# A hybrid encoder layer on one core: filter network and normalised input in a fixed order at the start

## The chip, the cores and the metric

The kernel runs on one core of one Trainium2 chip. The core has a matrix engine (TensorE, PE in the profile, with its weight loads as PEld), a vector engine (VectorE, DVE), an activation engine (ScalarE, ACT), a general engine (GpSimd, POOL) and a queue that issues the DMAs here (SyncE, SP). Each works through its own instructions in the order in which they were written down at build time, and waits on semaphores for the others. The metric is the device time of one execution in microseconds (us); lower is better.

## The reference

One layer, applied to a prompt of 1024 tokens and to a sample of 512, both of width 1024, all in float32:

```python
h = rmsnorm(x, norm_g)
z = h @ w_in                                   # 1024 -> 4096
hy_in, hy_gate, att_qkv, att_gate = split(z)
x0, x1, vv = split(short_conv(hy_in))
kfilt = hyena_filter(L, ...)                   # depends on L and the weights only
y_hy  = rmsnorm(x0 * long_conv(x1 * vv, kfilt, hy_bias)) * silu(hy_gate)
y_att = rmsnorm(neighbourhood_attention(q, k, v)) * silu(att_gate)
return x + concat([y_hy, y_att]) @ w_out

def hyena_filter(L, ...):                      # a small network of positions
    z = [t, cos(f w), -sin(f w)]               # 33 features
    h = sin(fr1 * (z @ w1 + b1))
    h = sin(fr2 * (h @ w2 + b2))
    h = (h @ w3) * exp(-t |deltas|)            # forward and backward halves
```

## The kernel before, in words

Products in full float32 precision are made of three faster ones: each operand is split into a rounded high part and a low remainder (`whi`, `wlo` for weights, `hThi`, `hTlo` for the normalised, transposed input), and high-high, high-low and low-high are added. A weight block `wraw` (128x1024) is loaded by SP, its two halves rounded by ScalarE into `whi` and, in all stages, subtracted by GpSimd into `wlo` (line 365).

The order of the work within an engine is not that of the code: a scheduler sorts the instructions by priority and by a simulation of the engines at build time, and writes one list for each engine. A block under `high_priority(n)` goes ahead; a block under `manual_schedule(engines=...)` keeps, on the named engine, the order in which the code issues it.

The start does this for the prompt, in two segments of 512 tokens. Four 128x1024 tiles `x` arrive; ScalarE sums their squares (`xsq`, line 229); VectorE takes an inverse root of the four sums (`rsqrt`: a seed and three Newton steps on 128x4 elements, tiles `rs_h`, `rs_y`, `rs_t`); VectorE scales the four `x` (line 79); TensorE transposes 128x128 squares of them into PSUM banks, ScalarE rounds a bank into `hThi` and VectorE subtracts it into `hTlo` (line 75). The projections (line 404) of a segment then run, three matmuls to each of 8 depth blocks and 4 token blocks, first `k` and `q`, then `v` and the gates.

Beside it the filter network runs: features `z_p`, `z_s` times `w1` (line 164), a sine argument reduced to one turn by VectorE (tiles `arg`, `n`), a sine on ScalarE (line 178), the second layer the same way, and a split into `hm`. Then VectorE adds up transform matrices (`dftm` from `km`, `fc`) and splits `w3`. The next step, the K phase, multiplies `hm` by `w3` (line 552) and by the decay tables `dec` into `xk`, and transforms the result (tiles `zc`) into the filters' spectra, which are stored as `K_p` and `K_s`. It runs woven with the projections. Meanwhile the sample's rows `px` are normalised, turned into `hl`, and stored as `hT`. After it come the long convolution of the prompt, the prompt's attention with the sample's convolution, the sample's attention and the output product.

Of the kernel before, what the change touches and what calls it, by code (L numbers as in the profile page):

```python
# [9 lines left out]
F32 = mybir.dt.float32  # L10
F32R = mybir.dt.float32r
I32 = mybir.dt.int32
AF = mybir.ActivationFunctionType
ALU = mybir.AluOpType
AX = mybir.AxisListType

P = 128
D = 1024
KC = 8
# [15 lines left out]
def f32(ap):  # L35
    return ap.bitcast(F32)


class Group:
    def __init__(self, name, L, x, out, z2, dec, tw0):  # L40
        self.name, self.L, self.x, self.out, self.z2, self.dec = name, L, x, out, z2, dec
        self.nt = L // P
        self.rows = L // GW
        self.B = 2 * L // P
        self.half = self.B // 2
        self.tw0 = tw0
        self.nseg = L // 512


class Kernel:  # L50
# [49 lines left out]
    def setup(self):  # L100
        nc, io, ctx = self.nc, self.io, self.ctx
        g = self.gp = ctx.enter_context(self.pool("const"))
        self.wp = ctx.enter_context(self.pool("w"))
        self.w_pools = itertools.repeat(self.wp)
        self.w_round = itertools.repeat(nc.scalar.copy)
        self.psum_cm, self.pp = {}, {}
        self.w_pos, self.w_raw, self.w_ready, self.w_bufs = 0, [], [], 4
        self.dr = ctx.enter_context(self.pool("dr", space=bass.MemoryType.DRAM))

        self.ident = g.tile([P, P], F32, name="ident")  # L110
        make_identity(nc, self.ident)
        self.ones = g.tile([P, 1], F32, name="ones")
        nc.gpsimd.memset(self.ones, 1.0)
        self.pc = g.tile([P, 70], F32, name="pc")
        self.dma(self.pc, io["pconst"])
        o = 0
        names = [("norm_g", 8), ("cw0", 12), ("cw1", 12), ("cw2", 12), ("cb", 12), ("on_hy", 4), ("on_att", 4),
                 ("qg", 1), ("kg", 1), ("b1", 1), ("fr1", 1), ("b2", 1), ("fr2", 1)]
        self.v = {}
        for n, w in names:  # L120
            self.v[n] = self.pc[:, o:o + w]
            o += w
        self.gq = g.tile([P, 1], F32, name="gq")
        nc.scalar.mul(out=self.gq, in_=self.v["qg"], mul=-0.125)
        self.fc = g.tile([P, 4, P], F32, name="fc")
        self.F = {n: self.fc[:, i] for i, n in enumerate(["M1f", "M2f", "M1i", "M2i"])}

        self.A_d, self.ga_d, self.v_d, self.K_d, self.qk_d = {}, {}, {}, {}, {}
        self.sum_d = self.dr.tile([self.P_.L, D], F32, name="sum")
        self.hT_d = [self.dr.tile([P, KC, self.S_.L], F32, name=f"hT{a}") for a in range(2)]  # L130
        for G in (self.P_, self.S_):
            self.A_d[G.name] = [self.dr.tile([P, G.L], F32, name=f"A_{G.name}{i}") for i in range(8)]
            self.ga_d[G.name] = [self.dr.tile([P, G.L], F32, name=f"ga_{G.name}{i}") for i in range(4)]
            self.K_d[G.name] = [self.dr.tile([P, 2 * G.half + 1, P], F32, name=f"K_{G.name}{i}") for i in range(4)]
            self.qk_d[G.name] = {(n, i): self.dr.tile([G.L, 256], F32, name=f"{n}_{G.name}{i}") for n in "qk" for i in range(2)}
            nr = 16 if G.name == "p" else 9
            self.v_d[G.name] = [[self.dr.tile([nr * 40, 4, P], F32, name=f"v_{G.name}{i}{hf}") for hf in range(2)] for i in range(2)]

    def mlp_setup(self, fl, mp):
        io = self.io  # L140
        self.hm, self.z, self.w12 = {}, {}, []
        self.w3 = [fl.tile([P, HW], F32R, name=f"w3{n}") for n in ("f", "b", "lof", "lob")]
        for nm in ("w1", "w2"):
            self.w12.append(mp.tile([io[nm].shape[0], P], F32, name=nm))
        for G in (self.P_, self.S_):
            self.hm[G.name] = [fl.tile([P, G.L], F32R, name=f"hm{d}_{G.name}") for d in range(2)]
            self.z[G.name] = mp.tile([66, G.L], F32, name=f"z_{G.name}")

    def mlp_load(self):
        for w, nm in zip(self.w12, ("w1", "w2")):  # L150
            self.dma(w, self.io[nm])
        for G in (self.P_, self.S_):
            self.dma(self.z[G.name], G.z2)

    def filters_mlp(self, G, mp):
        nc = self.nc
        w1, w2 = self.w12
        h = self.z[G.name]
        for layer, (w, b, fr) in enumerate(((w1, "b1", "fr1"), (w2, "b2", "fr2"))):
            nxt = None if layer else mp.tile([P, G.L], F32, name=f"h1_{G.name}")  # L160
            for s in range(G.nseg):
                sl = slice(s * 512, (s + 1) * 512)
                ps = self.bank("ml")
                nc.tensor.matmul(ps, lhsT=w, rhs=h[:, sl], start=True, stop=True)
                arg = mp.tile([P, 512], F32, name="arg", bufs=2)
                self.ts(arg, ps, self.v[b], ALU.add, self.v[fr], ALU.mult)
                n = mp.tile([P, 512], F32, name="n", bufs=2)
                magic = 12582912.0
                self.ts(n, arg, 1.0 / TWO_PI, ALU.mult, magic, ALU.add)
                self.ts(n, n, magic, ALU.subtract)  # L170
                c1 = 6.28125
                c2 = 0.0019350051879882812
                c3 = TWO_PI - c1 - c2
                self.stt(arg, n, -c1, arg)
                self.stt(arg, n, -c2, arg)
                self.stt(arg, n, -c3, arg)
                self.ts(arg, arg, 3.1415925, ALU.min, -3.1415925, ALU.max)
                nc.scalar.activation(out=nxt[:, sl] if nxt else arg, in_=arg, func=AF.Sin)
                if layer:
                    self.stack([t[:, sl] for t in self.hm[G.name]], arg)  # L180
            h = nxt
            yield

    def stack(self, out, src):

# [16 lines left out]
    def rsqrt(self, pool, ss, n, scale, name):  # L202
# [6 lines left out]
        self.ts(y.bitcast(I32), y.bitcast(I32), -1, ALU.mult, 0x5F3759DF, ALU.add)  # L209
        for _ in range(3):  # L210
            self.mul(t, y, y)
            self.mul(t, t, h)
            self.ts(t, t, -0.5, ALU.mult, 1.5, ALU.add)
            self.mul(y, y, t)
        return y


    def x_norm(self, G, xp, ahead):

        nc = self.nc  # L220
        G.xs = []
        for s in range(G.nseg):
            ss = xp.tile([P, 4], F32, name="ss", bufs=2)
            for j in range(4):
                tt = s * 4 + j
                x = xp.tile([P, D], F32, name="x", bufs=G.nt)
                self.dma(x, G.x[tt * P:(tt + 1) * P, :])
                sq = xp.tile([P, D], F32, name="xsq", bufs=1)
                nc.scalar.activation(out=sq, in_=x, func=AF.Square, accum_out=ss[:, j:j + 1])
                G.xs.append(x)  # L230
                if ahead:
                    ahead.pop(0)()
            r = self.rsqrt(xp, ss, 4, 1.0 / D, "x")
            for j in range(4):
                x = G.xs[s * 4 + j]
                self.ts(x, x, r[:, j:j + 1])

    def x_turn(self, G, hps):

        nc = self.nc  # L240
        G.hi = [p.tile([P, KC, 512], F32R, name=f"hThi_{G.name}") for p in hps]
        G.lo = [p.tile([P, KC, 512], F32R, name=f"hTlo_{G.name}") for p in hps]
        for s in range(G.nseg):
            for k in range(KC):
                ps = self.bank()
                for j in range(4):
                    nc.tensor.transpose(out=ps[:, j * P:(j + 1) * P], in_=G.xs[s * 4 + j][:, k * P:(k + 1) * P], identity=self.ident)
                gk = self.v["norm_g"][:, k:k + 1]
                nc.scalar.activation(out=G.hi[s][:, k], in_=ps, func=AF.Copy, scale=gk)
                self.stt(G.lo[s][:, k], ps, gk, f32(G.hi[s][:, k]), ALU.subtract)  # L250

    def x_pre(self, G, pool):

# [99 lines left out]
    def issue_w(self):  # L353
# [6 lines left out]
        for u in range(2):  # L360
# [1 line left out]
            lo = pool.tile([P, 512], F32R, name="wlo", bufs=4)  # L362
            r = raw[:, u * 512:(u + 1) * 512]
            next(self.w_round)(out=hi, in_=r)  # L364
            nc.gpsimd.tensor_tensor(out=lo, in0=r, in1=f32(hi), op=ALU.subtract)  # L365
            self.w_ready.append((key, hi, lo))

    def take_w(self, key):
# [762 lines left out]
    def run(self):  # L1131
# [30 lines left out]
        sc, sp = opn("stage")  # L1162
        mc, mp = opn("mlp")
        self.mlp_setup(fl, mp)
        with self.tc.high_priority(4000):
            self.x_norm(Gp, xp, [lambda: None] * 3 + [self.issue_w] + [lambda: None] * 3 + [self.issue_w])
            self.x_turn(Gp, (hp0, hp1))
        self.mlp_load()
        for _ in zip(self.filters_mlp(Gp, mp), self.filters_mlp(Gs, mp)):
            pass  # L1170
        self.w3_load(mp)
        self.dft_load(self.fc, self.io["fconst"].rearrange("p (n a) c -> p n a c", a=2), sp, "fc")
        self.dft = self.dft_mats(kd, self.io["kmat"], range(1, 8), sp, ("km0", "km1"))
# [211 lines left out]
```

## Time and profile before

| what | us |
|---|---|
| three runs | 1089.95, 1091.8, 1094.8 |
| their median | 1091.8 |
| the profiled execution | 1090.92 |
| its span between first and last instruction | 1089.1 |
| TensorE busy in the span | 1003.6 |
| VectorE / ScalarE / GpSimd busy | 800.1 / 463.1 / 415.5 |

The profiled execution takes 1.8 us more than its span, and 0.9 us less than the median. TensorE is busy for 92% of the span; the first of the 40 slices (27 us each) shows it busy for three tenths and the second for eight. A busy share counts an instruction until its modelled end, so that consecutive matmuls overlap; the rate at which they start is read from their start times.

### The profile page before, as it was taken

What the parts mean: (1) busy time and instruction counts of PE and PEld (TensorE: products, weight loads), DVE (VectorE), ACT (ScalarE), POOL (GpSimd) and SP (SyncE); (2) the same over time, 40 slices, a digit from 0 to 9 for tenths busy, and PEclk for the clock granted to TensorE, in tenths of its full rate; (3) what the DMA queues carried; (4) which work ended last, traced back from release to release, by engine and by line L of the source; (5) the groups of instructions that cost most, each with busy time, mean ns of one, the idle gap of its engine ahead of it and who ended that gap; (6) DMA issues with size and microseconds to landing.
All of it is one profiled execution on the core that took longest, in us unless ns stands there. A gap on an engine that the chain in (4) does not pass through costs nothing.

```text
span 1089.1 us, 18072 instructions
## 1 busy us (share of the span) xinstructions
PE 1003.6 (92%) x6444; PEld 906.6 (83%) x6444; DVE 800.1 (73%) x2134; ACT 463.1 (43%) x958; POOL 415.5 (38%) x336
## 2 busy tenths in 40 slices
PE   3898999988999999999989999987989989899997
PEld 2698999977788888888877887876968879899987
DVE  5997779552157767967559999887967977587874
ACT  6453334233331323122124565655747653476530
POOL 2032332112142323123256344354254356784651
PEclk9999999999999999999989999999999999999999
DMA  8226372756312121212483354435544478966522
GB/s 299 69 78 195 119 235 91 242 161 241 109 39 80 58 62 58 67 54 92 173 240 106 94 145 130 129 100 168 141 133 115 132 237 263 295 183 211 173 72 97
DMA packets 112216, 154.84 MB, mean 142 GB/s; under 512 B 7953, under 2 KB 80475, under 8 KB 111615
## 3 DMA queue, kind: packets, MB, share of 16 engines
q1 hardware_dynamic: 112127, 153.69, 45.3%
q8 instruction: 51, 0.84, 0.3%
q14 instruction: 38, 0.31, 0.1%
HBM read 110.35 MB, written 43.32 MB: 141 GB/s over the span
## 4 chain that ended last, share of the span: by engine, by line
PE 48%; DVE 27%; DMA 12%; issue 5%; ACT 4%; SPq 2%; POOL 1%; POOLq 0%; DVEq 0%; ACTq 0%
PE bank L391 25%; PE bank L1094 7%; PE bank L443 3%; PE bank L404 3%; DMA dec<-in_dec_p_dram 2%; PE bank L1012 2%; SPq L60 2%; DVE zc L63 2%; DMA v_p<-vg 2%; DMA v_s<-vg 2%; PE bank L445 2%; PE bank L444 2%; DVE s_sb L981 2%; PE bank L1003 2%; DVE s L63 1%
## 5 line engine op out<-in xcount | busy, mean ns | idle before, releaser
L365 POOL TENSOR_TENSOR wlo<-wraw,whi 128x512 fp32r<-128x512 f32 x160 | 233.7, 1464 | 514.3 <-ACT whi L364 322.5
L391 PE MATMUL bank<-hThi_p,whi 128*128 128x512 f32 x320 | 126.8, 396 | 3.9 <-DVE vg L63 3.2
L391 PE MATMUL bank<-hThi_p,wlo 128*128 128x512 f32 x320 | 126.7, 396 | 0.0
L391 PE MATMUL bank<-hTlo_p,whi 128*128 128x512 f32 x320 | 126.3, 395 | 0.0
L404 PE MATMUL bank<-whi,hThi_p 128*128 128x256 f32 x384 | 111.6, 293 | 6.3 <-DVE vg L63 3.2
L1094 PE MATMUL bank<-whi,hi 128*128 128x256 f32 x384 | 111.6, 292 | 6.0 <-ACT oo L1106 2.6
L1094 PE MATMUL bank<-whi,lo 128*128 128x256 f32 x384 | 110.7, 292 | 0.9 <-POOL lo L63 0.9
L1094 PE MATMUL bank<-wlo,hi 128*128 128x256 f32 x384 | 110.9, 290 | 0.0
L404 PE MATMUL bank<-wlo,hThi_p 128*128 128x256 f32 x384 | 110.6, 289 | 0.0
L404 PE MATMUL bank<-whi,hTlo_p 128*128 128x256 f32 x384 | 108.4, 287 | 0.0
L985 ACT ACTIVATE s_sb<-s_sb,mx 128x360 f32<-128x360 f32 (+1 forms) x96 | 60.3, 629 | 88.2 <-DVE mx L981 87.8
L364 ACT CAST whi<-wraw 128x512 fp32r<-128x512 f32 x66 | 40.9, 623 | 108.0 <-PE bank L391 72.9
L1094 PEld LDWEIGHTS bank<-whi,hi 128*128 128x128 f32 x384 | 75.4, 196 | 7.4 <-ACT oo L1106 2.8
L404 PEld LDWEIGHTS bank<-whi,hThi_p 128*128 128x128 f32 x384 | 74.2, 194 | 8.2 <-DVE vg L63 3.7
L364 DVE CAST whi<-wraw 128x512 fp32r<-128x512 f32 x94 | 58.6, 626 | 27.6 <-POOL lo L63 6.8
L1094 PEld LDWEIGHTS bank<-whi,lo 128*128 128x128 f32 x384 | 74.6, 196 | 1.6 <-POOL lo L63 1.6
L404 PEld LDWEIGHTS bank<-wlo,hThi_p 128*128 128x128 f32 x384 | 74.5, 194 | 1.0 <-issue 1.0
L1094 PEld LDWEIGHTS bank<-wlo,hi 128*128 128x128 f32 x384 | 75.2, 196 | 0.0
L391 PEld LDWEIGHTS bank<-hThi_p,whi 128*128 128x128 f32 x320 | 60.4, 189 | 17.1 <-DVE vg L63 4.1
L404 PEld LDWEIGHTS bank<-whi,hTlo_p 128*128 128x128 f32 x384 | 73.3, 193 | 0.3 <-issue 0.2
L391 PE MATMUL bank<-hThi_s,whi 128*128 128x512 f32 x160 | 65.6, 413 | 8.4 <-DVE vg L63 4.9
L1012 PE MATMUL bank<-pt,V 120*64 120x256 f32 (+1 forms) x352 | 66.5, 295 | 6.6 <-DVE pt L63 4.2
(279 smaller groups left out, 2765.8 us busy)
## 6 DMA issues: line engine op xcount, KB each, us to landing
wraw<-in_w_ch_dram SPq DMA_DIRECT2D x40, 512.0 KB
wraw<-in_w_tk_dram SPq DMA_DIRECT2D x24, 512.0 KB
wraw<-in_w_out_dram SPq DMA_DIRECT2D x16, 512.0 KB
V<-v_p SPq DMA_DIRECT2D x32, 240.0 KB
v_p<-vg SPq DMA_DIRECT2D x32, 160.0 KB
K_p<-Kw SPq DMA_DIRECT2D x4, 1088.0 KB
x<-in_x_prompt_dram SPq DMA_DIRECT2D x8, 512.0 KB
dec<-in_dec_p_dram SPq DMA_DIRECT2D x16, 256.0 KB
```

The source lines that it names most:

```text
L60: eng.dma_start(out=out, in_=in_)
L63: (eng or self.nc.vector).tensor_tensor(out=out, in0=a, in1=b, op=op)
L364: next(self.w_round)(out=hi, in_=r)
L365: nc.gpsimd.tensor_tensor(out=lo, in0=r, in1=f32(hi), op=ALU.subtract)
L391: nc.tensor.matmul(ps, lhsT=w, rhs=h[s][:, k], start=(k == 0 and i == 0), stop=(k == KC - 1 and i == 2))
L404: nc.tensor.matmul(pss[t // 2][:, t % 2, :], lhsT=h[t // 4][:, k, t % 4 * P:(t % 4 + 1) * P], rhs=w, start=(k == 0 and i == 0 and t % 2 == ...
L443: mm(o, lhsT=c, rhs=z, start=True, stop=False)
L444: mm(o[:, 0:P], lhsT=ns if inverse else s, rhs=z[:, 1], start=False, stop=False)
L445: mm(o[:, P:], lhsT=s if inverse else ns, rhs=z[:, 0], start=False, stop=True)
L985: nc.scalar.activation(out=s_sb[:, :n], in_=s_sb[:, :n], func=AF.Exp, bias=mx, scale=-1.0, accum_out=l)
L1012: nc.tensor.matmul(o, lhsT=vl, rhs=pr_, start=(c == 0 and i == 0), stop=(c == ncu - 1 and i == 1))
L1094: nc.tensor.matmul(ps[:, j, :], lhsT=h[:, tok], rhs=w, start=(k == 0 and i == 0 and j == 0), stop=(k == 3 and i == 2 and j == 1))
```

## The change

The filter network is cut into a function for one layer and one segment (`mlp_seg`). The features of the prompt with `w1` and `w2` are loaded ahead of `x`; the first layer's first segment is issued ahead of the normalisation. The whole opening stands under a fixed order for VectorE: first-layer segment 0, root and scaling of the first `x` segment, a weight block, its `hTlo`, then the second `x` segment in the same way, then two more first-layer segments. The second layer follows outside. The first weight block's two low parts are made by VectorE, all later ones by GpSimd. A Newton step of the root is three instructions and no longer four, and the sine argument's reduction takes two subtractions in place of three.

```diff
+        self.w_low = itertools.chain([nc.vector] * 2, itertools.repeat(nc.gpsimd))
...
-                c2 = 0.0019350051879882812
-                c3 = TWO_PI - c1 - c2
-                self.stt(arg, n, -c1, arg)
-                self.stt(arg, n, -c2, arg)
-                self.stt(arg, n, -c3, arg)
+        self.stt(arg, n, -c1, arg)
+        self.stt(arg, n, c1 - TWO_PI, arg)
...
             self.mul(t, y, y)
-            self.mul(t, t, h)
-            self.ts(t, t, -0.5, ALU.mult, 1.5, ALU.add)
-            self.mul(y, y, t)
+            self.stt(t, t, -0.5, h, ALU.mult)
+            self.stt(y, t, 1.5, y, ALU.mult, ALU.add)
...
-            nc.gpsimd.tensor_tensor(out=lo, in0=r, in1=f32(hi), op=ALU.subtract)
+            self.sub(lo, r, f32(hi), next(self.w_low))
...
-        with self.tc.high_priority(4000):
-            self.x_norm(Gp, xp, [lambda: None] * 3 + [self.issue_w] + [lambda: None] * 3 + [self.issue_w])
-            self.x_turn(Gp, (hp0, hp1))
-        self.mlp_load()
-        for _ in zip(self.filters_mlp(Gp, mp), self.filters_mlp(Gs, mp)):
-            pass
+        with self.tc.high_priority(4000), self.tc.manual_schedule(engines={self.nc.vector.engine}):
+            self.mlp_load(Gp)
+            self.mlp_seg(Gp, mp, 0, 0)
+            self.x_norm(Gp, 0, xp)
+            self.issue_w()
+            self.x_turn(Gp, 0, hp0)
+            self.x_norm(Gp, 1, xp)
+            self.issue_w()
+            self.x_turn(Gp, 1, hp1)
+            self.mlp_load(Gs)
+            self.mlp_seg(Gp, mp, 0, 1)
+            self.mlp_seg(Gs, mp, 0, 0)
+        for G, sg in ((Gp, 0), (Gp, 1), (Gs, 0)):
+            self.mlp_seg(G, mp, 1, sg)
```

The instructions move as follows. First, VectorE's list around the second segment's root, before; `rs_..._249` to `251` are that root, `km` a transform matrix as loaded, `bank` a PSUM bank:

```order
L75 SCALAR_TENSOR_TENSOR hTlo_p<-bank,pc,hThi_p 128x512
L63 TENSOR_TENSOR dftm<-km_507 128x256
L75 SCALAR_TENSOR_TENSOR arg<-n,arg 128x512
L63 TENSOR_TENSOR rs_t_251<-rs_t_251,rs_h_249 128x4
L75 SCALAR_TENSOR_TENSOR arg<-n,arg 128x512
L63 TENSOR_TENSOR dftm<-km_511 128x256
L75 SCALAR_TENSOR_TENSOR arg<-n,arg 128x512
L81 TENSOR_SCALAR rs_t_251<-rs_t_251 128x4
L75 SCALAR_TENSOR_TENSOR arg<-n,arg 128x512
L63 TENSOR_TENSOR dftm<-km_515 128x256
```

The same place now, from the last Newton steps of that root (`rs_..._311` to `313`) to the second segment's low parts:

```order
L64 TENSOR_TENSOR rs_t_313<-rs_y_312 128x4
L76 SCALAR_TENSOR_TENSOR rs_t_313<-rs_t_313,rs_h_311 128x4
L76 SCALAR_TENSOR_TENSOR rs_y_312<-rs_t_313,rs_y_312 128x4
L64 TENSOR_TENSOR dftm<-km_506 128x256
L64 TENSOR_TENSOR rs_t_313<-rs_y_312 128x4
L76 SCALAR_TENSOR_TENSOR rs_t_313<-rs_t_313,rs_h_311 128x4
L76 SCALAR_TENSOR_TENSOR rs_y_312<-rs_t_313,rs_y_312 128x4
L80 TENSOR_SCALAR x<-x,rs_y_312 128x1024 x4
L76 SCALAR_TENSOR_TENSOR hTlo_p<-bank,pc,hThi_p 128x512 x8
L82 TENSOR_SCALAR arg<-bank,pc 128x512
```

Before, sine arguments stand between the steps of the root; now only `dftm` additions do, and the sine arguments (`arg`) of the other segments follow behind all of `hTlo`.

Second, ScalarE's list at the very start, before; `gq` is a small constant, `xsq` the squares of one `x` tile:

```order
L124 ACTIVATE gq<-pc 128x1
L229 ACTIVATE xsq,ss<-x 128x1024 x4
L364 CAST whi<-wraw 128x512 x4
L229 ACTIVATE xsq,ss<-x 128x1024 x3
L249 ACTIVATE hThi_p<-bank,pc 128x512 x3
```

And now:

```order
L126 ACTIVATE gq<-pc 128x1
L225 ACTIVATE xsq,ss<-x 128x1024 x3
L178 ACT_TABLE_LOAD
L178 ACTIVATE h_p<-arg 128x512
L225 ACTIVATE xsq,ss<-x 128x1024
L361 CAST whi<-wraw 128x512 x4
L225 ACTIVATE xsq,ss<-x 128x1024 x3
L246 ACTIVATE hThi_p<-bank,pc 128x512 x3
```

A table load and the first sine now stand between the third and the fourth square.

Third, SP's list of DMA issues from the sample's first rows (`px`) on, before; `k_p` is a store of finished keys, `hT` one of turned sample rows, `dec` a load of a decay table:

```order
L60 DMA px<-in_x_sample_dram 128x1024
L60 DMA wraw<-in_w_tk_dram 128x1024 x2
L60 DMA dec<-in_dec_p_dram 128x512 x2
L60 DMA hyb<-in_hy_bias_dram 1x128
L60 DMA dec<-in_dec_p_dram 128x512 x2
```

And now:

```order
L61 DMA px<-in_x_sample_dram 128x1024
L61 DMA wraw<-in_w_tk_dram 128x1024 x2
L61 DMA k_p_96<-raw_824 128x8x256
L61 DMA wraw<-in_w_tk_dram 128x1024
L61 DMA hT_76<-hl 128x4x128
L61 DMA dec<-in_dec_p_dram 128x512 x2
```

The first two `dec` loads have moved behind a store of keys, a weight load and a store of sample rows.

## Rows read from the trace of the kernel before

**Rows 1.** Windows: length, busy us (count) of PE, PEld, DVE, ACT, POOL; clock; DMA.

```profile
38.50:48.30 9.80, 5.01 (x17) 2.53 (x17) 8.95 (x22) 3.70 (x6) 0.00 (x0) 0.83 0.13 51
...
77.00:106.00 29.00, 26.06 (x208) 25.15 (x209) 20.35 (x53) 9.66 (x21) 8.91 (x7) 1.00 0.62 200
```

**Rows 2.** Timeline, TensorE: start, duration, line, tiles, count, idle before.

```profile
18.10 2.80 PE L247 MATMUL bank<-ident,x 128*128 128x128 f32 x12 [18.10 <-DVE x L79]
21.26 0.58 PE L404 MATMUL bank<-whi,hThi_p 128*128 128x256 f32 x1 [0.35 <-ACT hThi_p L249]
...
23.68 0.28 PE L404 MATMUL bank<-whi,hThi_p 128*128 128x256 f32 x1
23.80 0.28 PE L404 MATMUL bank<-wlo,hThi_p 128*128 128x256 f32 x1
...
33.12 1.02 PE L164 MATMUL bank<-z_s,w 66*128 66x512 f32 x2
...
42.67 2.07 PE L164 MATMUL bank<-h_p,w 128*128 128x512 f32 x2 [4.21 <-DVE arg L81]
45.08 2.45 PE L247 MATMUL bank<-ident,x 128*128 128x128 f32 x12 [0.33 <-DVE x L79]
...
48.26 0.68 PE L404 MATMUL bank<-whi,hThi_p 128*128 128x256 f32 x1
...
106.26 1.03 PE L458 MATMUL bank<-zc,fc 128*128 128x256 f32 x4
```

**Rows 3.** Timeline, GpSimd and VectorE, the first root and scaling.

```profile
10.82 4.94 POOL L365 TENSOR_TENSOR wlo<-wraw,whi 128x512 fp32r<-128x512 f32 x4 [9.51 <-ACT whi L364]
10.89 1.22 DVE L63 TENSOR_TENSOR rs_t<-rs_t,rs_h 128x4 f32<-128x4 f32 x1
...
16.41 0.16 DVE L63 TENSOR_TENSOR rs_t<-rs_y 128x4 f32<-128x4 f32 x1
...
17.20 2.74 DVE L79 TENSOR_SCALAR x<-x,rs_y 128x1024 f32<-128x1024 f32 x4
```

**Rows 4.** Timeline, ScalarE and SP: fourth square, casts, first sine, first `dec`.

```profile
8.90 1.06 ACT L229 ACTIVATE xsq<-x 128x1024 f32<-128x1024 f32 x1
...
10.12 2.42 ACT L364 CAST whi<-wraw 128x512 fp32r<-128x512 f32 x4
...
39.85 1.28 ACT L178 ACT_TABLE_LOAD   x1
41.15 1.15 ACT L178 ACTIVATE h_p<-arg 128x512 f32<-128x512 f32 x2
...
70.87 0.90 SPq L60 DMA_DIRECT2D dec<-in_dec_p_dram  x2
...
84.94 0.39 SPq L60 DMA_DIRECT2D hT<-hl  x1
```

**Rows 5.** Window of VectorE alone: length, busy us (count), clock, DMA share, GB/s.

```profile
17.20:44.20 27.00, 24.56 (x58) 0.97 0.46 158
```

**Rows 6.** VectorE's groups, 17.2 to 44.1 us: count, busy us, mean ns, idle before.

```profile
L75 DVE SCALAR_TENSOR_TENSOR arg<-n,arg 128x512 f32<-128x512 f32 x7 | 4.8, 681 | 0.0
...
L79 DVE TENSOR_SCALAR x<-x,rs_y 128x1024 f32<-128x1024 f32 x4 | 2.7, 750 | 0.0
L81 DVE TENSOR_SCALAR arg<-bank,pc 128x512 f32<-128x512 f32 x3 | 2.4, 805 | 0.8 <-ACT h_p L178 0.8
...
L81 DVE TENSOR_SCALAR n<-arg 128x512 f32<-128x512 f32 x3 | 1.3, 420 | 0.0
```

**Rows 7.** Timeline, VectorE: the second segment's scaling, first and eighth `xk`.

```profile
44.19 2.74 DVE L79 TENSOR_SCALAR x<-x,rs_y 128x1024 f32<-128x1024 f32 x4
...
77.34 0.68 DVE L63 TENSOR_TENSOR xk<-bank,dec 128x512 f32<-128x512 f32 x1
...
94.92 0.69 DVE L63 TENSOR_TENSOR xk<-bank,dec 128x512 f32<-128x512 f32 x1 [2.05 <-DMA dec<-in_dec_p_dram]
```

**Rows 8.** Waits of TensorE, whole span: total us, times, longest.

```profile
PE bank L404 <- ACT qsq L825: 2.6, 2, 2.3
```

More of the change, by code (lines that the diff above doesn't have):

```diff
@@ L42, in __init__ @@
         self.nt = L // P
+        self.xs, self.hi, self.lo = [], [], []
         self.rows = L // GW
@@ L140, in mlp_setup @@
         io = self.io
-        self.hm, self.z, self.w12 = {}, {}, []
+        self.hm, self.z, self.h1, self.w12 = {}, {}, {}, []
         self.w3 = [fl.tile([P, HW], F32R, name=f"w3{n}") for n in ("f", "b", "lof", "lob")]
@@ L147, in mlp_setup, with mlp_load @@
             self.z[G.name] = mp.tile([66, G.L], F32, name=f"z_{G.name}")
[L149 to L152, printed above, removed]
+    def mlp_load(self, *gs):
+        for G in gs:
             self.dma(self.z[G.name], G.z2)
-    def filters_mlp(self, G, mp):
+            for w, nm in zip(self.w12, ("w1", "w2")) if G is self.P_ else ():
+                self.dma(w, self.io[nm])
+            self.h1[G.name] = None
@@ L156, in filters_mlp, with mlp_seg @@
+    def mlp_seg(self, G, mp, layer, s):
         nc = self.nc
[L157 to L171, printed above, removed]
-                c2 = 0.0019350051879882812
-                c3 = TWO_PI - c1 - c2
-                self.stt(arg, n, -c1, arg)
-                self.stt(arg, n, -c2, arg)
-                self.stt(arg, n, -c3, arg)
[L177 to L182, printed above, removed]
@@ new lines, in mlp_seg @@
+        w, b, fr = self.w12[layer], self.v[f"b{layer + 1}"], self.v[f"fr{layer + 1}"]
+        sl = slice(s * 512, (s + 1) * 512)
+        if not layer and not s:
+            self.h1[G.name] = mp.tile([P, G.L], F32, name=f"h1_{G.name}")
+        h = self.h1[G.name] if layer else self.z[G.name]
+        ps = self.bank("ml")
+        nc.tensor.matmul(ps, lhsT=w, rhs=h[:, sl], start=True, stop=True)
+        arg = mp.tile([P, 512], F32, name="arg", bufs=2)
+        self.ts(arg, ps, b, ALU.add, fr, ALU.mult)
@@ new lines, in mlp_seg @@
+        n = mp.tile([P, 512], F32, name="n", bufs=2)
+        magic = 12582912.0
+        self.ts(n, arg, 1.0 / TWO_PI, ALU.mult, magic, ALU.add)
+        self.ts(n, n, magic, ALU.subtract)
+        c1 = 6.28125
+        self.stt(arg, n, -c1, arg)
+        self.stt(arg, n, c1 - TWO_PI, arg)
+        self.ts(arg, arg, 3.1415925, ALU.min, -3.1415925, ALU.max)
+        nc.scalar.activation(out=arg if layer else self.h1[G.name][:, sl], in_=arg, func=AF.Sin)
+        if layer:
+            self.stack([t[:, sl] for t in self.hm[G.name]], arg)
@@ L211, in rsqrt, with x_norm @@
             self.mul(t, y, y)
-            self.mul(t, t, h)
-            self.ts(t, t, -0.5, ALU.mult, 1.5, ALU.add)
-            self.mul(y, y, t)
+            self.stt(t, t, -0.5, h, ALU.mult)
+            self.stt(y, t, 1.5, y, ALU.mult, ALU.add)
         return y
-    def x_norm(self, G, xp, ahead):
+    def x_norm(self, G, s, xp):
         nc = self.nc
-        G.xs = []
-        for s in range(G.nseg):
-            ss = xp.tile([P, 4], F32, name="ss", bufs=2)
-            for j in range(4):
[L225 to L250, printed above, removed]
+        ss = xp.tile([P, 4], F32, name="ss", bufs=2)
@@ new lines, in x_norm @@
+        xs = []
+        for j in range(4):
+            tt = s * 4 + j
+            x = xp.tile([P, D], F32, name="x", bufs=G.nt)
+            self.dma(x, G.x[tt * P:(tt + 1) * P, :])
+            sq = xp.tile([P, D], F32, name="xsq", bufs=1)
+            nc.scalar.activation(out=sq, in_=x, func=AF.Square, accum_out=ss[:, j:j + 1])
+            xs.append(x)
+        if not s:
+            self.fetch_w()
+        r = self.rsqrt(xp, ss, 4, 1.0 / D, "x")
+        for j in range(4):
+            self.ts(xs[j], xs[j], r[:, j:j + 1])
@@ new lines, in x_norm, with x_turn @@
+        G.xs += xs
+    def x_turn(self, G, s, hp):
+        nc = self.nc
+        hi = hp.tile([P, KC, 512], F32R, name=f"hThi_{G.name}")
+        lo = hp.tile([P, KC, 512], F32R, name=f"hTlo_{G.name}")
+        G.hi.append(hi)
+        G.lo.append(lo)
+        for k in range(KC):
+            ps = self.bank()
+            for j in range(4):
+                nc.tensor.transpose(out=ps[:, j * P:(j + 1) * P], in_=G.xs[s * 4 + j][:, k * P:(k + 1) * P], identity=self.ident)
+            gk = self.v["norm_g"][:, k:k + 1]
+            nc.scalar.activation(out=hi[:, k], in_=ps, func=AF.Copy, scale=gk)
+            self.stt(lo[:, k], ps, gk, f32(hi[:, k]), ALU.subtract)
```

## The prediction

> **What bounds the kernel now.** I read the slices of the page first: TensorE is busy for 92% of the span, and the only slices that fall far below that are the first two. So the start is where time lies open, and elsewhere a gain must take work or a gap from TensorE. The timeline of TensorE says where the open time is [rows 2]. It starts at 18.10, when the first scaled `x` is there, and projects from 21.26. Then comes a gap of 4.21 us before 42.67, a sine matmul pair that takes 2.07 where a pair at 33.12 took 1.02, and the second segment's transposes at 45.08. Its first projection starts at 48.26. In 38.5 to 48.3 TensorE is busy for 5.01 of 9.80 us, at a granted clock of 0.83 [rows 1], a mean of time at the low level, 1.2 GHz, in which the pair took 2.07, and at the full 2.4. What it waits for is VectorE: the second segment's scaling starts only at 44.19 [rows 7]. Between the two scalings, 27.0 us, VectorE is busy for 24.56 [rows 5], and a good part of that is sine arguments [rows 6], which stand between the steps of a root that takes almost nothing itself. After 48 TensorE runs without gaps to 77. In 77 to 106 it is idle for 2.9 us of 29 [rows 1], of which one wait of 2.3 is for a ScalarE instruction on finished keys [rows 8].
>
> **The start.** Before, the fourth square begins at 8.90 and ends, with its sum read out, at about 10.1 [rows 4]; the root begins there, and the first scaling at 17.20, 7.1 us later. Of this, four steps stood for some 1.2 us each, as long as one of GpSimd's four low parts (4.94 for four); undisturbed steps come every 0.2 us (four from 16.41 to 17.20) [rows 3].
>
> Now the features and two small matrices, 361 KB by their shapes, go ahead of `x`. An `x` tile of 512 KB arrives each 1.3 us or so, the pitch of the squares, so that they cost 0.9 by bytes, and 1.2 if three issues of 0.39 limit (that of `hT` [rows 4]). Behind the third square stand the table load and a sine. The load takes 1.28 and the sine starts 1.30 after the load's start; two sines take 1.15, so one about 0.6 [rows 4]. So the fourth square moves from 8.90 to about 8.9 + 1.0 + 1.3 + 0.6 = 11.8, if the argument is there by 11.2: loads from about 4, a matmul of 2.07 at the low clock and six VectorE instructions of 0.42 to 0.80 (3.2 in all) end near 10. The square ends at 13.05. Twelve steps at 0.2 would end at 15.5. But the second weight block's low parts stay with GpSimd. Its casts follow those of the first, 0.6 each [rows 4]; the first of the second block ends at 14.9, and GpSimd then runs 2.5 us into the root's last steps. As before, one step stands through each low part. I take that: the scaling starts at 17.7, 0.5 later than before. Without the meeting it would be 15.5, 1.7 earlier; a late sine argument could add 1. The two low parts that VectorE now makes (0.68 each by the like-shaped sine step [rows 6]) stand behind the scaling, beside the transposes, and are done before the first `hThi`'s matmul or shortly after it; they delay `hTlo` by about 0.5, for which TensorE has high-high and low-high products to do.
>
> On the table load the trace has 1.28 us, and 1.30 from its start to the sine's. The Trainium skill, ScalarE: Activation LUTs, section "What ACT_TABLE_LOAD costs", has 1283 ns for the load and another 1380 ns of drain for each switch, 2.66 in all. By that page the scaling would start 1.4 later still and my gain would be smaller by as much; the row shows no such drain between load and sine, so the sum goes by the row.
>
> **The second segment.** From the first scaling to the second VectorE took 27.0 us [rows 5]. Out of this stretch go 18 sine instructions. Consecutive starts are 0.08 closer than durations (four scalings of 0.750 take 2.74), so they are worth 7 x 0.60 + 3 x 0.72 + 8 x 0.34 = 9.1 us [rows 6], and with them the 0.8 that one waited for a sine. Into it come two low parts (1.3), and the root's steps, which now follow one another: 12 at up to 0.2 in place of 15 hidden between longer work, about 1.2 more. Also the `dftm` additions now stand between the root's steps and need `km` tiles whose two buffers are refilled one after another; before, nothing waited for them, since sine work lay between. I take 1.0, with bounds of 0 and 4.1, two waits such as the 2.05 in which the eighth `xk` stood for a load [rows 7]. Sum: 27.0 - 9.1 - 0.8 + 1.3 + 1.2 + 1.0 = 20.6. So the second scaling starts at 17.7 + 20.6 = 38.3 in place of 44.19. From scaling to projection took 4.06 both times (17.20 to 21.26, 44.19 to 48.26); so the second segment's projections start at 42.4 in place of 48.26, 5.9 earlier.
>
> That is not all gained. Three of the sine matmuls that TensorE had done by 48.26 are still ahead of it: before it had done five of six, now two. They cost at most 1.02 each [rows 2]: 3.1. What is left is 2.8. TensorE will end the first segment near 36.3 (21.7 + 17.2 less three matmuls of 0.86 by their starts) and wait some 2.5 us.
>
> **The K phase.** The wait of 2.3 for the keys' buffer [rows 8] came because the store `k_p` was issued behind `dec` loads. It now stands ahead of them, right when its product is ready, so I count this gap as gone: 2.3, with 0 as the other end. The price is the first `dec` load, issued at 70.87 before [rows 4], which now stands behind the stores of `k_p` and `hT`. The list puts the turned sample rows after about 311 projections; at 0.12 each (23.68 to 23.80 [rows 2]), with transposes and sine matmuls, TensorE is there near 76, and four pairs of ScalarE and VectorE steps end near 79. So the first `xk`, at 77.34 before [rows 7], comes near 82. But the list also has 544 projections ahead of the first `zc` matmul, where before it had 473, which started at 106.26. These 71 more are 8.5 us of work, and TensorE will be at that place near 107 to 109. `xk` to `zc` took 28.9 before, with the eighth `xk` held for 2.05 by its load; 82 + 26.9 = 109. So I count nothing lost here, with 5 us as the other end.
>
> **The rest.** One subtraction less for each of the six sine segments is 6 x 0.60 = 3.6 us of VectorE, and 18 roots lose three small steps each, 3 x 0.08 to 0.2 a root, so 4 to 11 us over the kernel. VectorE is busy for 800 of 1089 us, and TensorE seldom waits for it; I count 0.7 of it. The scheduler also writes another order for the two attention stages, with the same work; I count nothing, and plus or minus 5 in the range.
>
> **Sum.** 2.8 + 2.3 + 0.7 = 5.8 from 1090.92 of the profiled execution: 1085.1. The median of the runs shown is 0.9 above that execution, so 1086.0 there. As the order's noise has no sign and the start's price is taken at its dear end, I predict 1085.5.
>
> **Rivals.** *The K phase takes it back to nothing.* If `xk` keep their old pace from 82, `zc` is ready at 111 and TensorE waits 3 to 5 us: 1085.5 + 4.5 = 1090. For it: the eighth `xk` stood for its load. Against it: that one wait was 2.05 of those 17.6 us [rows 7], beside stores that are now issued ahead.
>
> *The K phase makes it slower.* The turned rows come out of TensorE about when the first `xk` starts, 77.34, and their store was issued at 84.94 [rows 4, 7], 7.6 later. If it takes that again, from 76, `dec` lands at 87, `zc` are ready near 115, and TensorE waits 7 us; the next pair's `dec` loads stand behind stores in the same way and cost as much again once: 1085.5 + 14 - 5 (the second meets slack) = 1094.5. It decides from a first `xk` later than 84. Against it: before, VectorE's `xk` stood between those steps, and now they stand ahead of the first.
>
> *The opening is worth all of it.* If the root escapes GpSimd (1.7 + 0.5 = 2.2 more) and the 8.5 us of work that the list draws ahead of `zc` is all saved, 8.5 in place of 5.1: 1085.5 - 2.2 - 3.4 = 1080.
>
> *It doesn't do what it says:* the sine comes late and holds the fourth square, so that the scaling starts at 19 or later and the start is slower by 2: 1087.5, held within the forecast's own range.
>
> **How the numbers follow.** Forecast, 1082.5 to 1088.5 about 1085.5: 0.46. K phase to nothing, near 1090: 0.21. Slower, near 1094.5: 0.17. Worth all of it, near 1080: 0.16. About 0.5% (5.5 us) is what a measurement of this kernel can tell from no change, so faster means below 1086.3 and slower above 1097.3. Below 1086.3 lie six tenths of the forecast (0.28), the last case (0.16) and, from a better order in attention, 0.08: 0.52. Above 1097.3 lie 0.12, from the slow case with an unlucky order. The rest is 0.36. The range 1077 to 1096 leaves out about 0.1 on either side.
>
> **What would show it.** First scaling at 17 to 18.5, with one or two root steps of 1.2 beside GpSimd; second scaling at 37 to 39.5 with no sine work ahead of it; TensorE's second gap 2 to 3 us and the clock near 1 through 38 to 48; first `xk` at 80 to 83; `zc` on TensorE at 106 to 109. I am wrong if the second scaling comes after 42, if the first `xk` comes after 84, or if the gain at 110 us is there and gone by the end.

## The result, and the profile after

The changed kernel takes 1081.48 us (median of 4 runs, 1081.17 to 1081.95) against 1092.12 for the kernel before on the same chip: ratio 0.990, 95% interval 0.9871 to 0.993. In a second set of runs it was 0.988 (0.9846 to 0.9915). The profiled execution took 1081.17, its span is 1079.4.

The start came as the edit says, but later than forecast. ScalarE's first square before, and then the answer to [rows 4], its timeline after:

```profile
4.98 1.06 ACT L229 ACTIVATE xsq<-x 128x1024 f32<-128x1024 f32 x1 [2.16 <-DMA x<-in_x_prompt_dram]
```

```profile
7.95 1.06 ACT L225 ACTIVATE xsq<-x 128x1024 f32<-128x1024 f32 x1 [5.17 <-DMA x<-in_x_prompt_dram]
...
11.79 1.28 ACT L178 ACT_TABLE_LOAD   x1
13.08 0.63 ACT L178 ACTIVATE h_p<-arg 128x512 f32<-128x512 f32 x1
13.62 1.04 ACT L225 ACTIVATE xsq<-x 128x1024 f32<-128x1024 f32 x1
```

The fourth square starts 4.7 later than before: 3.0 because the tiles of `x` land later (the first square shows it: 4.98 and 7.95), and 1.7 more behind table load and sine. Then GpSimd's and VectorE's timelines, answering to [rows 3, 7]:

```profile
16.38 2.53 POOL L64 TENSOR_TENSOR wlo<-wraw,whi 128x512 fp32r<-128x512 f32 x2 [15.08 <-ACT whi L361]
16.58 1.12 DVE L64 TENSOR_TENSOR rs_t<-rs_y 128x4 f32<-128x4 f32 x1
17.73 1.20 DVE L76 SCALAR_TENSOR_TENSOR rs_t<-rs_t,rs_h 128x4 f32<-128x4 f32 x1
...
19.16 2.74 DVE L80 TENSOR_SCALAR x<-x,rs_y 128x1024 f32<-128x1024 f32 x4
...
38.88 0.42 DVE L64 TENSOR_TENSOR dftm<-km 128x256 f32<-128x256 f32 x1 [0.96 <-DMA km<-in_kmat_dram]
...
39.81 2.74 DVE L80 TENSOR_SCALAR x<-x,rs_y 128x1024 f32<-128x1024 f32 x4
```

Two root steps stand through GpSimd's two low parts; the second scaling follows 20.65 after the first. TensorE's timeline, answering to [rows 2], with the first transposes of the convolution (`cx`) as the last row, and behind it that row before:

```profile
20.06 2.80 PE L244 MATMUL bank<-ident,x 128*128 128x128 f32 x12 [9.91 <-DVE x L80]
...
23.22 0.39 PE L401 MATMUL bank<-whi,hThi_p 128*128 128x256 f32 x1 [0.35 <-ACT hThi_p L246]
...
40.71 2.80 PE L244 MATMUL bank<-ident,x 128*128 128x128 f32 x12 [2.61 <-DVE x L80]
...
43.86 0.39 PE L401 MATMUL bank<-whi,hThi_p 128*128 128x256 f32 x1 [0.35 <-ACT hThi_p L246]
...
116.30 2.05 PE L455 MATMUL bank<-zc,fc 128*128 128x256 f32 x4 [4.43 <-DVE zc L64]
...
315.44 1.03 PE L609 MATMUL bank<-ident,cx 128*128 128x128 f32 x8
```

```profile
313.72 1.03 PE L612 MATMUL bank<-ident,cx 128*128 128x128 f32 x8
```

The second segment's projections start 4.4 earlier than before. But before had its first `zc` at 106.26 without a wait [rows 2], and its convolution began at 313.72: 1.7 earlier than now. The windows that answer to [rows 1]:

```profile
38.50:48.30 9.80, 7.18 (x47) 6.25 (x48) 6.76 (x13) 3.67 (x7) 0.00 (x0) 0.83 0.06 25
77.00:106.00 29.00, 26.22 (x216) 25.61 (x215) 21.94 (x43) 10.56 (x23) 11.34 (x10) 1.00 0.67 207
```

TensorE gained 2.2 of busy time in 38 to 48, at the same granted clock of 0.83 as before, and next to none in 77 to 106. Its wait for the keys' squares, which answers to [rows 8]:

```profile
PE bank L401 <- ACT qsq L822: 2.4, 1, 2.4
```

The wait at 95.48 is gone, but one as long now stands at 171.61. And SP's and VectorE's timelines of the K phase, answering to [rows 4, 7]:

```profile
80.36 0.39 SPq L61 DMA_DIRECT2D k_p<-raw  x1
86.39 0.38 SPq L61 DMA_DIRECT2D hT<-hl  x1
86.86 0.96 SPq L61 DMA_DIRECT2D dec<-in_dec_p_dram  x2
...
90.61 0.69 DVE L64 TENSOR_TENSOR xk<-bank,dec 128x512 f32<-128x512 f32 x1 [2.04 <-DMA dec<-in_dec_p_dram]
```

The first `dec` load is 16 later than before.

So where is the gain? From the convolution's first transposes to the end of the span before took 1089.1 - 313.72 = 775.4, and now 1079.4 - 315.44 = 764.0. So 11.4 are gained behind the convolution's start and 1.7 lost ahead of it. The granted clock behind that point is 0.98 in both. The windows show TensorE busier in 700 to 800, inside the prompt's attention, and by 10.4. Before, and then after:

```profile
700.00:800.00 100.00, 85.92 (x560) 76.54 (x558) 81.00 (x211) 54.82 (x115) 39.56 (x33) 0.98 0.49 132
```

```profile
700.00:800.00 100.00, 96.36 (x630) 87.61 (x629) 90.03 (x235) 63.97 (x135) 47.30 (x40) 0.98 0.52 149
```

The sample's gated values `vg` explain the largest piece. They have one buffer, which four stores `v_s` empty before ScalarE may write it again. Timelines of SP, ScalarE and TensorE, before:

```profile
745.72 1.41 SPq L60 DMA_DIRECT2D v_s<-vg  x3
747.22 0.57 SPq L60 DMA_DIRECT2D qkr<-in_rpb_dram  x1
747.84 0.53 SPq L60 DMA_DIRECT2D v_s<-vg  x1
...
756.03 0.59 ACT L845 CAST vg<-bank 128x512 fp32r<-128x512 f32 x1 [5.87 <-DMA v_s<-vg]
757.39 0.39 PE L404 MATMUL bank<-whi,hThi_s 128*128 128x256 f32 x1 [2.28 <-DVE vg L63]
...
786.92 1.41 SPq L60 DMA_DIRECT2D v_s<-vg  x3
788.42 0.57 SPq L60 DMA_DIRECT2D qkr<-in_rpb_dram  x1
789.09 0.46 SPq L60 DMA_DIRECT2D wraw<-in_w_ch_dram  x1
789.61 12.93 SPq L60 DMA_DIRECT2D v_s<-vg  x5
...
798.95 0.59 ACT L845 CAST vg<-bank 128x512 fp32r<-128x512 f32 x1 [7.89 <-DMA v_s<-vg]
800.31 0.68 PE L391 MATMUL bank<-hThi_s,whi 128*128 128x512 f32 x1 [4.92 <-DVE vg L63]
```

And after:

```profile
750.70 0.59 ACT L842 CAST vg<-bank 128x512 fp32r<-128x512 f32 x1 [3.38 <-DMA v_s<-vg]
...
781.92 2.37 SPq L61 DMA_DIRECT2D v_s<-vg  x4
...
786.85 0.59 ACT L842 CAST vg<-bank 128x512 fp32r<-128x512 f32 x1 [2.60 <-DMA v_s<-vg]
787.32 0.36 SPq L61 DMA_DIRECT2D wraw<-in_w_ch_dram  x1
```

Before, the fourth store stood behind a load of a bias table of 244 KB, the second time behind a weight load of 512 KB too. It released ScalarE 8.2 after its own issue the first time (747.84 to 756.03) and 9.3 the second (789.61, the first of the five in that row, to 798.95); VectorE and TensorE stood behind ScalarE. Now the four stores stand together, ahead of the weight load, and ScalarE goes on 3.5 after the fourth one's issue (783.38 to 786.85). The two TensorE waits, 2.28 and 4.92, are gone: 7.2 of the 11.4.

The rest of it is not a sum of smaller waits. From the convolution's start on, TensorE's idle time falls from 46.2 to 39.5, by 6.7, so that its other waits together grew a little. The remaining 4.7 is busy time, 729.15 before and 724.46 after for the same matmuls, and what makes it shorter is not shown.

### The profile page after: what moved, and what is told of

It is laid out like the page before. It is cut to its first block, busy times and chain, and to the rows that moved or that the text cites. A ratio compares the mean times of both kernels' runs of the same rounds, so it can differ in the third digit from the quotient of the medians.

```text
span 1079.4 us, 18013 instructions
## 1 busy us (share of the span) xinstructions
PE 1001.2 (93%) x6444; PEld 908.1 (84%) x6444; DVE 797.3 (74%) x2076; ACT 460.3 (43%) x958; POOL 416.0 (39%) x334
## 4 chain that ended last, share of the span: by engine, by line
PE 60%; DVE 20%; DMA 9%; ACT 4%; issue 3%; POOL 2%; SPq 1%; DVEq 0%; ACTq 0%; POOLq 0%
PE bank L388 27%; PE bank L1091 9%; PE bank L401 6%; PE bank L440 4%; PE bank L1009 2%; PE bank L442 2%; PE bank L441 2%; PE bank L1000 2%; DVE zc L64 1%; DVE whi L361 1%; SPq L61 1%; DMA dec<-in_dec_p_dram 1%; DVE s_sb L978 1%; DMA qkr<-in_rpb_dram 1%; DVE rs_t L76 1%
## 5 line engine op out<-in xcount | busy, mean ns | idle before, releaser
L361 DVE CAST whi<-wraw 128x512 fp32r<-128x512 f32 x94 | 60.8, 653 | 21.6 <-PE bank L388 7.3
L388 PEld LDWEIGHTS bank<-hTlo_p,whi 128*128 128x128 f32 x320 | 60.6, 189 | 12.1
L388 PEld LDWEIGHTS bank<-hThi_p,wlo 128*128 128x128 f32 x320 | 60.4, 189 | 11.9
```

Of the source, the lines that this page charges most:

```text
L388: nc.tensor.matmul(ps, lhsT=w, rhs=h[s][:, k], start=(k == 0 and i == 0), stop=(k == KC - 1 and i == 2))
```

## The experiments

Three groups, each on one chip beside the kernel before, whose medians there were 1094.95 (opening alone, shorter root alone, both shorter steps, x first), 1091.81 (late roots old and short, two old steps, second layer inside) and 1092.84 (the other four). A ratio is to the kernel before of the same group. The fourth column is the start of the convolution's transposes, the last is what remains of the span from there; both are from one profiled execution of each kernel, and the changed kernel's two profiles differ by 1.9 and 0.8 in them:

| kernel | median us | ratio (95%) | convolution at | rest |
|---|---|---|---|---|
| before | 1092.12 | 1 | 313.7 | 775.4 |
| changed | 1081.48 | 0.990 (0.9871 to 0.993) | 315.4 | 764.0 |
| opening alone | 1091.79 | 0.9974 (0.9949 to 0.9998) | 317.6 | 772.2 |
| late roots old | 1087.9 | 0.9959 (0.9936 to 0.9983) | 311.5 | 774.7 |
| shorter root alone | 1073.61 | 0.979 (0.9751 to 0.9828) | 309.2 | 765.6 |
| the same again | 1075.69 | 0.9833 (0.98 to 0.9867) | 308.5 | 765.3 |
| both shorter steps | 1083.14 | 0.9893 (0.9855 to 0.9931) | 318.7 | 761.5 |
| late roots short | 1079.64 | 0.989 (0.985 to 0.993) | 317.3 | 760.7 |
| two old steps | 1079.24 | 0.9883 (0.9847 to 0.992) | 318.0 | 763.4 |
| x first | 1076.96 | 0.9835 (0.9799 to 0.9871) | 313.9 | 759.9 |
| second layer inside | 1079.44 | 0.9872 (0.9841 to 0.9904) | 313.2 | 764.7 |
| four tables ahead | 1073.73 | 0.9818 (0.9784 to 0.9852) | 310.6 | 762.1 |
| x first, four tables | 1073.75 | 0.9822 (0.9787 to 0.9858) | 306.7 | 760.9 |
| changed, again | 1079.88 | 0.988 (0.9846 to 0.9915) | 313.5 | 763.2 |

The theory after the result: the gain is made in attention, by the order that the scheduler writes there once a root has fewer instructions; the opening's lead is lost before the convolution. The rival: the opening makes the gain.

**Opening alone**: the changed kernel with the old root and the old sine reduction. The root's part of the edit:

```diff
-            self.stt(t, t, -0.5, h, ALU.mult)
-            self.stt(y, t, 1.5, y, ALU.mult, ALU.add)
+            self.mul(t, t, h)
+            self.ts(t, t, -0.5, ALU.mult, 1.5, ALU.add)
+            self.mul(y, y, t)
```

> The changed kernel with the old root (four instructions a Newton step) and the old sine argument (three subtractions); the opening's order, its loads and the two low weights on VectorE as changed. From the convolution on, TensorE's list is that of the kernel before, instruction by instruction. Theory 1 (the gain is made in the attention stages by the shorter root and the order that comes with it; the opening's lead is lost again before the convolution): 1091 to 1095 us, the convolution's first transposes 0 to 4 us later than before's 313.7. Theory 2 (the opening is what gains): 1081 to 1086 us.

1091.79, a gain of 0.3%, and the rest is long, 772.2 against 775.4 before. The rival falls: the opening alone does not make the change's 1%.

**Shorter root alone**: the kernel before with that diff the other way round, nothing else.

> The kernel before with the shorter root alone, everywhere; opening, loads, low weights and sine argument as before. From the convolution on, TensorE's list is that of the changed kernel. Theory 1: 1079 to 1084 us, with the attention stage 9 to 13 us shorter and the convolution's start within 3 us of before's. Theory 2: 1089 to 1092 us.

1073.61: a gain of 2.1%, more than that of the whole change, and more than the 1079 to 1084 expected; the convolution starts 4.5 earlier than before, not within 3. Run again beside the changed kernel it was 1075.69 against 1079.88.

> The kernel before with the shorter Newton step everywhere and nothing else of the change, beside the changed kernel. If the late roots' order is the whole gain and the opening's other edits cost time: 5 to 9 below the changed kernel, 1072 to 1077. If the 7.9 us between the two medians so far were the chips' difference: within 2 of it.

> The changed kernel beside the other three. 1080 to 1083, ratio 0.99, by both theories; it is the base for the differences.

The difference is 4.2 there, below the 5 to 9 expected, and the intervals of the two ratios overlap slightly. The place agrees: the rest is equal (765.3 and 763.2), and the convolution starts 5.0 earlier without the opening.

**Both shorter steps**: the kernel before with the shorter root and the two-step sine reduction.

> The kernel before with the shorter root and the shorter sine argument. TensorE's list in the attention stage is that of the changed kernel but for nine rows, in the output stage it is a third one. Theory 1: 1078 to 1086 us; a gain in the attention stage as in the shorter root alone, the output stage free to differ by some us either way. Theory 2: 1088 to 1092 us.

1083.14. The rest is short (761.5), but the convolution starts at 318.7. With the shorter sine argument the order of K phase and projections is another one, and the kernel is 9.5 slower than with the root alone.

**X first**: the changed kernel, with `x` loaded first and the network's first segment behind the second segment's root.

```diff
-            self.mlp_load(Gp)
-            self.mlp_seg(Gp, mp, 0, 0)
             self.x_norm(Gp, 0, xp)
...
             self.x_norm(Gp, 1, xp)
+            self.mlp_load(Gp)
+            self.mlp_seg(Gp, mp, 0, 0)
```

> The changed kernel with the features and the first layer's first segment behind the second segment's scaling in the opening's order, so that x loads first again and no sine stands ahead of the fourth square. If the loads and the sine cost what the profile shows (first square 3.0 us and first scaling 2.0 us later than before), the first scaling comes near 15.5 to 16.5 in place of 19.2 and the first projection 3 us sooner. Theory 1 (what the opening wins is lost in the K phase): the whole moves by less than 2 us from the changed kernel's 1081.5, apart from another order in the output stage (some us either way): 1078 to 1086. Theory 2 (an early start is kept to the end): 1077 to 1079.

The first projection comes at 18.6, 4.6 earlier than in the changed kernel, and the convolution at 313.9, within the 313.5 to 315.4 of the changed kernel's two profiles. The start's 4.6 do not reach it. By 48 us TensorE has started 186 matmuls where the changed kernel has started 177, so little of the lead is left, and later it waits at the same place for the same thing, as its timeline shows:

```profile
115.85 2.05 PE L455 MATMUL bank<-zc,fc 128*128 128x256 f32 x4 [5.12 <-DVE zc L64]
```

The median, 1076.96, lies below both expectations; in the profile what is shorter is the rest (759.9).

**Late roots short, late roots old.** The first is the kernel before with the shorter step only where the root is not that of `x`; the second the changed kernel with the old step there.

```diff
+            if name != "x":
+                self.mul(t, y, y)
+                self.stt(t, t, -0.5, h, ALU.mult)
+                self.stt(y, t, 1.5, y, ALU.mult, ALU.add)
+                continue
```

> The kernel before with the shorter Newton step in the roots of the attention stages alone (all roots but those of x): opening and K phase are word for word those of before. If the late roots and the order that they bring make the gain: convolution within 1 us of before (313.7), 820 us marker 10 to 20 earlier, median 1074 to 1080. If the gain of the shorter root came from the roots of x at the start: no change, 1090 to 1095.

> The changed kernel with the four-instruction step back in the attention stages' roots; opening, sine and the roots of x stay changed. TensorE's list from the convolution on is then that of before. If late roots make the gain: no gain is left, 1089 to 1094, convolution near 315 as in the changed kernel, and waits such as the 4.92 us near 800 us back. If the opening makes it: 1081 to 1084.

1079.64 and 1087.9: the late roots carry most of the gain in either direction. With the old ones 0.4% of gain is left, and 1087.9 lies just below the 1089 to 1094 expected. The start of the convolution missed both expectations by 3.5 (317.3 and 311.5), so the part before it varies by itself. ScalarE's timeline in late roots old has the old waits:

```profile
752.18 0.59 ACT L848 CAST vg<-bank 128x512 fp32r<-128x512 f32 x1 [6.01 <-DMA v_s<-vg]
...
795.19 0.59 ACT L848 CAST vg<-bank 128x512 fp32r<-128x512 f32 x1 [7.98 <-DMA v_s<-vg]
```

and in late roots short there are the new ones:

```profile
751.43 0.59 ACT L850 CAST vg<-bank 128x512 fp32r<-128x512 f32 x1 [3.44 <-DMA v_s<-vg]
...
787.92 0.59 ACT L850 CAST vg<-bank 128x512 fp32r<-128x512 f32 x1 [2.76 <-DMA v_s<-vg]
```

TensorE in 700 to 800 follows: 85.35 busy in the one, 95.17 in the other. In all fourteen profiles the store's place and the rest go together: in the three with the old late roots the fourth store stands behind the bias table, ScalarE waits 5.9 to 6.3 and 7.9 to 8.1 for it, and TensorE is idle for 44 to 47 us of the rest; in the other eleven the four stores stand together, ScalarE waits at most 4.5, and TensorE is idle for 38 to 41. That the place of the fourth store is the cause is read from these traces; a kernel that moves this store alone was not run.

**Two old steps**: the kernel before with `range(2)` for `range(3)` in the root; the third step is left out.

> The kernel before with two of the root's three Newton steps (the third is left out, so the root is less exact), each of four instructions: 8 instructions in a root, where before has 12 and the shorter step 9. TensorE's list from the convolution on is that of the kernel with the shorter root alone. If the order is what counts: as that kernel, 1071 to 1077. If the number of VectorE instructions counts: 4/3 of its gain of 21 us, 1064 to 1069.

1079.24, not the 1064 to 1069 that fewer instructions alone would give. With the list of the shorter root its rest is 763.4 (765.6 there). It missed 1071 to 1077 too: its convolution starts 8.8 later. This speaks for the order and against the number of steps.

**Second layer inside**: the changed kernel with the second layer's prompt segments in VectorE's fixed order.

```diff
             self.mlp_seg(Gp, mp, 0, 1)
+            self.mlp_seg(Gp, mp, 1, 0)
+            self.mlp_seg(Gp, mp, 1, 1)
...
```

> The changed kernel with the second layer's two prompt segments within VectorE's fixed order, so that the first decay loads are issued ahead of the store of the sample's turned rows again. If the late first decay load takes the opening's lead back: first xk near 77, first zc matmul near 106, convolution near 309 (6 earlier than 315.4), median 1074 to 1077. If the lead is lost at another place (the tail of the projections): zc early, convolution within 2 us of 315, median 1080 to 1083.

The edit missed its aim: the first `xk` comes at 93.89, later than in the changed kernel. The first decay loads stand ahead of `hT` now, but behind two weight loads, as SP's timeline shows:

```profile
76.47 0.39 SPq L61 DMA_DIRECT2D k_p<-raw  x1
77.73 12.04 SPq L61 DMA_DIRECT2D wraw<-in_w_tk_dram  x2
89.86 0.86 SPq L61 DMA_DIRECT2D dec<-in_dec_p_dram  x2
```

SP's waits in 66 to 93 name the cause:

```profile
SPq L61 <- POOL wlo L64: 12.1, 2, 11.3
```

A weight load waits for GpSimd's low part, and all loads of the queue stand behind it. So this run decides nothing on the K phase.

**Four tables ahead**: the changed kernel with four decay tables loaded early, in tiles of their own.

```diff
+        self.dec_first = []
+        for q in range(4):
+            self.dec_first.append(fl.tile([P, 2, 256], F32, name=f"dec{q}"))
+            self.dma(self.dec_first[-1], Gp.dec[0][:, q * 2:(q + 1) * 2, :])
...
-                fetch()
+                if len(decs) < 2:
+                    fetch()
```

> The changed kernel with the first four decay tables loaded into tiles of their own ahead of the transform matrices, so that the first four products xk no longer stand behind the stores of keys and turned rows. If the late decay load takes the opening's lead back: first xk near 81 (90.6 in the changed kernel), TensorE's wait of 4.43 before the first zc matmul below 1, convolution at 309 to 312 (315.4), median 4 to 6 below the changed kernel in the same runs. If the lead is lost in the tail of the projections whatever xk do: the wait before zc goes, waits on Kw and vg between 200 and 290 grow, convolution within 1.5 of 315.4, median within 2 of the changed kernel.

1073.73, 6.2 below the changed kernel in the same runs. VectorE's and TensorE's timelines:

```profile
88.20 1.88 DVE L64 TENSOR_TENSOR xk<-bank,dec 128x512 f32<-128x512 f32 x3
...
107.21 1.03 PE L455 MATMUL bank<-zc,fc 128*128 128x256 f32 x4
```

The first `xk` is only 2.4 earlier, not the 9.6 expected: VectorE still finishes the late second layer (`hm_p`, until 83.7) and the turned rows first. But three follow at once, the first `zc` matmul comes 9.1 earlier, its wait is gone, and the convolution starts 3.0 to 4.9 earlier than in the changed kernel's two profiles. So the wait for `zc` was a real loss, and it can be had back; the rest of the 6.2 is not divided up.

**X first and four tables** together:

> As the kernel with four decay tables ahead, and with x loaded first and the network's first segment behind the second segment's root, as in the kernel with x first (1076.96). If start and K phase both count and add up: 4 to 6 below that one, 1071 to 1073. If the lead is lost in the tail of the projections: 1075 to 1079, as x first alone.

1073.75 (1069.34 to 1078.46), between the two ranges expected. The profile has the earliest convolution of all (306.7) and a span of 1067.5, but the median does not tell this kernel from four tables alone or from the shorter root alone. These three, near 1074 to 1076, are ahead of both kernels.

## Why the prediction was right or wrong

It said 1085.5 and faster by about half a percent; it was 1081.5 and a full percent. The direction was right, but for a reason that the sum had put at nothing. That the time came out so near is luck: of what the sum did count nothing is left at the convolution, and the opening alone gained 0.3%.

*The start*, forecast at 17.7 for the first scaling, came at 19.16. The step that failed is the price of the loads ahead of `x`: 1.0 by bytes and issues, 3.0 measured. SP issues the first `x` 1.2 later (2.41 for 1.19), and in 3 to 5 us the DMA engines move 224 GB/s where before they moved 383. The scaling came at 19 or later, as in the last rival, but not for its reason: the sine's argument was ready at 10.9, before the table load at 11.79. Table load to sine took 1.29, so the sum was right to go by the row. The drain of which the Trainium skill speaks, in ScalarE: Activation LUTs, section "What ACT_TABLE_LOAD costs", does not show here either. Two root steps beside GpSimd came as counted.

*The second segment.* 20.6 between the scalings was forecast, 20.65 measured; the waits for `km`, taken as 1.0, were 2.28 in three, with less elsewhere. TensorE's second gap is 2.61 (2.5 forecast), and the lead at the projections is 4.4 in place of 5.9, all of the difference from the start. One sign failed: the granted clock in 38 to 48 was to be near 1 and is 0.83, as before.

*The K phase* failed. I counted the keys' wait of 2.3 as gone; one of 2.4 stands at 171.61 instead. I counted nothing lost behind the later `dec`; the load came at 86.86 (the turned rows ahead of it were to end near 79), the first `xk` at 90.61 (82), `zc` at 116.3 (106 to 109). A first `xk` later than 84 was named as the point where the slower rival decides, and as a sign of being wrong. That rival's mechanism did come true: `dec` at 87 and `zc` near 115 were its numbers. Its price did not: TensorE waited 4.43 and not 7, and the convolution starts 1.7 later. But the lead is gone. At 106 us TensorE had started 613 matmuls where before it had 587; then came the wait, and behind it a stretch at the low level, 1.2 GHz: the granted clock is 0.50 in 115.4 to 118.6, and the first four `zc` matmuls take 2.05 where before they took 1.03 [rows 2]. TensorE did turn the first rows at 76.5, as counted. What was left out is VectorE's list: its next step on them, forecast to follow at once, stands behind the second layer, whose sine arguments and `hm_p` the opening has pushed back. VectorE's timeline, after:

```profile
78.02 1.41 DVE L64 TENSOR_TENSOR hm_p<-arg,hm_p 64x512 fp32r<-64x512 f32 x1
79.46 1.42 DVE L76 SCALAR_TENSOR_TENSOR arg<-n,arg 128x512 f32<-128x512 f32 x1
80.91 1.67 DVE L64 TENSOR_TENSOR hm_p<-arg,hm_p 64x512 fp32r<-64x512 f32 x1
...
83.22 0.35 DVE L76 SCALAR_TENSOR_TENSOR hl<-bank,pc,hl 128x128 fp32r<-128x128 f32 x1
```

Three of these steps take 1.4 to 1.7 here, where a sine step took 0.68 [rows 6], and the first low part `hl` starts at 83.22.

*The rest.* The new order in attention was put at nothing, plus or minus 5. It measured 11.4, and the runs put it on the late roots: with fewer instructions in them the rest of the span is 759.9 to 765.6 in eleven profiles (the changed kernel's two among them), with the old ones 772.2 to 775.4 in three. The sum's 2.8 + 2.3 + 0.7 was in truth about -1.7 to 0.2 before the convolution and 11 to 12 behind it. The matmuls were the same; what I failed to do was to read the new list against the waits of before, where ScalarE stood 5.87 and 7.89 for `v_s`.

Open is why the part before the convolution moves by as much as 12 us (306.7 to 318.7) between lists that hold nearly the same work. TensorE's idle time ahead of it runs from 33 to 43 in the fourteen profiles. The traces show waits of TensorE for `vg`, `Kw` and `zc` that come and go there, and only that for `zc` was tested. An early `zc` alone does not do it: both shorter steps has its first `zc` matmul at 96.24, 10 earlier than before, and the latest convolution of all.

## What to carry to other kernels

Where a scheduler writes the order, a shorter helper can change every stage that calls it: compare the lists of the far stages too, and time such an edit alone before it is joined to others. Follow a lead to the next chain of loads and stores: it is worth only what that chain lets through. A tile with one buffer, emptied by several stores, is as fast as the last of them, so look at what stands between them in the queue.

## What the runs showed of the hardware

A store of 160 KB issued behind a load of 244 KB and, 0.5 before it, one of 512 KB on the same queue released the engine that waited to write its tile again 9.3 after its issue; behind the load of 244 KB alone it was 8.2. With four such stores issued one behind the other (781.92 to 784.29) it was 3.5 after the fourth one's issue. Loads of 361 KB ahead of `x` moved its tiles by 3.0, over three times what their bytes at the tiles' pitch would take; 1.2 of it was the issue of the three loads.
